# Stores on the queues of ScalarE and GpSimd, and sums products by contraction at two seams of a transformer block

## The chip, the cores and the metric

The kernel runs on one core of one Trainium2 chip. The metric is the device time of one execution in microseconds. Engines: PE is TensorE (matrix products), PEld its weight loads, DVE is VectorE, ACT is ScalarE, POOL is GpSimd, SP is SyncE, which up to now issues nearly all DMAs.

## The reference, cut to what matters

One layer of a hybrid block on a sequence of 1024 tokens with 1024 channels, all in 32-bit floats. The input is normalised and multiplied with one wide matrix w_in. Three branches follow: retention (4 heads), gated linear attention (4 heads) and sliding-window attention (16 query heads). They are projected, gated, summed, projected again and added to the input; then comes a gated feed-forward of width 2816.

```python
for l in range(DEPTH):                      # DEPTH = 1
    h = rmsnorm(x, norm_mix_pre[l])
    proj = h @ w_in[l]
    ...                                     # o_ret, o_gla, o_swa from slices of proj
    branches = jnp.stack([o_ret, o_gla, o_swa], axis=2)
    projected = jnp.einsum('bsnc,ncd->bsnd', branches, w_branch[l])
    gates = jax.nn.sigmoid(gate_logits.reshape(B, S, N_BRANCH, D_MODEL))
    merged = jnp.sum(gates * projected, axis=2)
    x = x + rmsnorm(merged @ w_out[l], norm_mix_post[l])
    h = rmsnorm(x, norm_ffn_pre[l])
    f = (jax.nn.silu(h @ ffn_w_gate[l]) * (h @ ffn_w_up[l])) @ ffn_w_down[l]
    x = x + rmsnorm(f, norm_ffn_post[l])
```

## The kernel before, in words

Every operand of a product is split into a high part (a cast on ScalarE, line 113) and a remainder (a subtraction, mostly on VectorE, line 114), and each product is three matmuls: high by high, high by low, low by high. `split` does this, `moving` does it into a new tile.

The stages follow one another in the listing. First the norm of x and its transposes; then the sliding-window branch, whose softmax steps are interleaved with projections (`swa_scores`, `swa_scale`, `swa_probs_t`, `swa_out`, up to some 325 us); then the eight heads of the two linear branches (`lin_head` and the functions around it, up to 784 us). Along the heads GpSimd also makes sums of blocks of the transposed input in `h_sums`, which are stored to DRAM as `tsum` and loaded again later.

Two stages then compute pairs of weight columns as 2 x 2 block products with seven products in place of eight: the class `Pairs`. It is used first for the gates (`gates`, 18 keys, a lead of 2 pairs) and later for the feed-forward's gate and up products (`up`, 22 keys, a lead of 3). For a key n the blocks a11, a12, a21, a22 come from two weight tiles `raw`. `blocks` splits the upper two, `sums` makes the sums s1 to s4 and splits s2 and s3, and `split` the others. The products are p1 (a11 by b11, into x), p2 (a12 by b21, into y), p6 (s2 by t2, onto x), p5 (s1 by t1, into z), p7 (s3 by t3, onto x), p4 (a22 by t4, onto x) and p3 (s4 by b22, onto z), each four contraction steps of three matmuls of 512 columns. `out` combines the results: in the gates `gate_out` (Silu or Sigmoid on ScalarE; for the six keys of heads a load of `on` and a product on VectorE at line 981; a store at line 982), in the feed-forward `up_out` (a store of fT at line 1166).

`Pairs.steps` writes the order out by hand. For the first `lead` keys it goes product by product: p1 and p2 of each key, then p6 of each, p5 of each, p7 of each, and so on; afterwards key by key. Two seams lead into these stages. At the first, the gates follow the last head, and the sums t1 to t4 are loaded from DRAM at line 989, sixteen loads of 512 KB. At the second, the output projection (`out_mm`, tiles t = 0 to 7), the norm of each tile (`out_norm`), the transposes of the normed tile (`out_transpose`, 64 copies h2f on ScalarE at line 1118) and the first feed-forward products are interleaved by hand; t2 and t1 are made there by `h2_t2` and `h2_t1`, when the last tile has been transposed.

The last stage is the down product (`down_load`, `down_mm`): for each half of the tokens it loads rows of w_down and of fT, and after the last block of each half it norms and stores four tiles of the output at line 1255.

The listing is not exactly the order in which an engine runs: the framework orders the instructions of each engine by priority (their place in the listing) and by its own estimate of when their inputs are ready, and adds the semaphores. Each engine and each DMA queue then runs its instructions in that order. SBUF tiles come from two pools: 18 of 512 columns (`bt`, `br_`) and 45 of 1024 (`dt_`, `bpair`, `raw_tile`, `wt_pair`). PSUM has eight banks of 512 columns (`bank`).

Of the kernel before, what the change touches and what calls it, by code (L numbers as in the profile page):

```python
# [16 lines left out]
P = 128  # L17
# [49 lines left out]
def block_kernel(ctx: ExitStack, tc: tile.TileContext, x, vecs, rows, alpha2, w_in, w_branch,  # L67
# [44 lines left out]
    def split(hi, lo, src, eng=None):  # L112
        se.copy(out=hi, in_=src)  # L113
        (eng or ve).tensor_tensor(out=lo, in0=src, in1=hi, op=ALU.subtract)  # L114
# [323 lines left out]
    def swa_out(i, pts):  # L438
# [13 lines left out]
        if n % 2 == 1:  # L452
            for c in range(2):
                sp.dma_start(out=oT[2][g * 2 + c][:, (n // 2) * 256:(n // 2 + 1) * 256], in_=oo[0][:, c, :])
# [154 lines left out]
    def lin_out(br, h, th, y, sgs):  # L609
        for i in range(2):  # L610
# [6 lines left out]
            if sgs is None:  # L617
# [5 lines left out]
                sp.dma_start(out=oN[br][c][:, th * TH:(th + 1) * TH], in_=ot)  # L623
# [8 lines left out]
            sp.dma_start(out=oT[br][c][:, th * TH:(th + 1) * TH], in_=ot)  # L632
# [128 lines left out]
    def h_sums(k):  # L761
# [7 lines left out]
        for n, src in (("t2", t2), ("t3", t3), ("t1", b22), ("t4", b21)):  # L769
            pr = dt_(n, F32R)  # L770
            split(pr[:, :TH], pr[:, TH:], src)
            sp.dma_start(out=tsum[n][k], in_=pr.bitcast(F32))
# [27 lines left out]
    class Pairs:  # L800
# [5 lines left out]
        def __init__(self, mv, keys, load, out, lead):  # L806
            self.mv, self.keys, self.load, self.out, self.lead = mv, keys, load, out, lead
            self.raw, self.ops, self.x, self.z, self.sn = {}, {}, {}, {}, {}
# [28 lines left out]
        def product(self, n, ps, a, b, start):  # L837
            wh, wl = self.ops[n].pop(a)
            if callable(self.mv[b]):
                self.mv[b] = self.mv[b]()  # L840
            for k, (hi, lo) in enumerate(self.mv[b]):
                h, l = wh[:, k * P:(k + 1) * P], wl[:, k * P:(k + 1) * P]
                pe.matmul(ps, lhsT=h, rhs=hi, start=(start and k == 0), stop=False, skip_group_check=True)  # L843
                pe.matmul(ps, lhsT=h, rhs=lo, start=False, stop=False, skip_group_check=True)  # L844
                pe.matmul(ps, lhsT=l, rhs=hi, start=False, stop=(k == KH - 1), skip_group_check=True)  # L845
# [6 lines left out]
        def p2(self, n):  # L852
            y = bank("y")
            self.product(n, y, "a12", "b21", True)
            self.out(n, 0, 0, y, self.sn[n].pop())
# [22 lines left out]
        def steps(self):  # L878
            keys, lead = self.keys, self.lead
            first = keys[:lead]  # L880
            self.fetch(lead)
            for i, n in enumerate(first):
                self.blocks(n)
                self.p1(n)
                yield
                self.p2(n)
                if i == 0:
                    self.sums(n)
                yield
            for i, n in enumerate(first):  # L890
                if i:
                    self.sums(n)
                self.p6(n)
                yield
            self.fetch(lead + 1)
            for n in first:
                self.split(n, "s1")
                self.p5(n)
                yield
            for n in first:  # L900
                self.p7(n)
                yield
            if lead < len(keys):
                self.blocks(keys[lead])
                self.p1(keys[lead])
                yield
            for n in first:
                self.split(n, "a22")
                self.p4(n)
                yield  # L910
            self.fetch(lead + 2)
            if lead < len(keys):
                self.p2(keys[lead])
                yield
            for i, n in enumerate(first):
                self.split(n, "s4")
                if i == len(first) - 1 and lead < len(keys):
                    self.sums(keys[lead])
                    self.split(keys[lead], "s1")
                self.p3(n)  # L920
                yield
# [47 lines left out]
    def gate_out(n, row, th, ps, add):  # L969
# [12 lines left out]
        sp.dma_start(out=(gT if gate else oT)[br][c + row][:, t], in_=g)  # L982
# [105 lines left out]
    def out_norm(t, ps, eng):  # L1088
# [8 lines left out]
        sp.dma_start(out=x1d[t], in_=x1)  # L1097
# [7 lines left out]
    def out_transpose(t, xn):  # L1105
# [5 lines left out]
        for k0 in range(0, NK, 4):  # L1111
# [14 lines left out]
    def h2_t2():  # L1126
        res = []
        for k in range(KH):
# [3 lines left out]
            res.append(moving("t2", t2))  # L1132
            tsums.append((t3, t2))
        return res
# [155 lines left out]
```

## Time and profile before

| | |
|---|---|
| median of 3 runs | 2230.48 us (2230.38 to 2238.79) |
| profiled execution | 2228.47 us, its span 2226.6 us, mean clock of TensorE 0.984 |
| busy time | PE 2141.1 us, PEld 1809.9, DVE 1188.7, ACT 867.2, POOL 215.8 |
| DMA | 274.32 MB, mean 123 GB/s, nearly all issued by SP |

The profiled execution is one run, 2.0 us under the median; the span is what the trace covers of it. A busy TensorE is not one at its peak: matmuls are pipelined, and a 512-column matmul that lasts 0.39 us in the trace starts 0.23 us after the one before it. At half clock (1.2 in place of 2.4 GHz, "0.50" in the granted clock) the distance is 0.43 us. The clock shown for a stretch is the mean of the two levels.

### The profile page before, as it was taken

The numbers are of one execution on the slowest core, as the hardware profiler recorded it, in microseconds if no ns is written. First come the engines' busy times: TensorE is split into PE (matmuls) and PEld (weight loads), VectorE is DVE, ScalarE is ACT, GpSimd is POOL, SyncE is SP. The second block draws the span as 40 slices with busy tenths as digits, with TensorE's granted clock in tenths as the row PEclk, the third lists the DMA queues.
The fourth block names the chain that finished last, engine by engine and source line by source line (L and its number), as shares of the span: only waits on it lengthen the run. The fifth ranks groups of instructions, "written<-read, shape, count | busy, mean of one in ns | idle before, by whom it ended". The sixth has DMA issues, their size and how long they took to land. (4 is left out here: it accounts for less than half of the span.)

```text
span 2226.6 us, 28111 instructions
## 1 busy us (share of the span) xinstructions
PE 2141.1 (96%) x10792; PEld 1809.9 (81%) x10792; DVE 1188.7 (53%) x2222; ACT 867.2 (39%) x1664; POOL 215.8 (10%) x244
## 2 busy tenths in 40 slices
PE   7999999999999969999999999996999999999998
PEld 6888889998889958888888888874788888888786
DVE  4699966766654446544532344334755555544351
ACT  4477643444443324444441220253433333343240
POOL 3221013333111100000000000030000000000000
PEclk9999999999999989999999999998899999999999
DMA  4011121122211358655462551232164444484450
GB/s 158 10 48 39 58 77 69 67 68 92 86 57 57 123 198 251 208 170 170 147 231 100 170 179 63 84 123 92 46 181 137 138 142 142 123 292 142 151 199 38
DMA packets 291845, 274.32 MB, mean 123 GB/s; under 512 B 11728, under 2 KB 240336, under 8 KB 291712
## 3 DMA queue, kind: packets, MB, share of 16 engines
q1 hardware_dynamic: 291664, 272.41, 37.6%
q8 instruction: 84, 1.38, 0.2%
q14 instruction: 49, 0.40, 0.1%
q0 software_dynamic: 48, 0.13, 0.0%
HBM read 212.73 MB, written 59.77 MB: 122 GB/s over the span
## 5 line engine op out<-in xcount | busy, mean ns | idle before, releaser
L114 DVE TENSOR_TENSOR wl<-raw,wh 128x1024 fp32r<-128x1024 f32 x138 | 168.4, 1221 | 164.8 <-ACT wh L113 88.1
L113 ACT CAST wh<-raw 128x1024 fp32r<-128x1024 f32 (+1 forms) x157 | 163.0, 1044 | 186.7 <-DMA raw<-in_w_branch 65.1
L226 PE MATMUL pf<-hT,wh 128*128 128x512 f32 x480 | 188.8, 393 | 3.6 <-DVE skl L114 1.8
L227 PE MATMUL pf<-hT,wh 128*128 128x512 f32 x480 | 188.3, 392 | 0.0
L229 PE MATMUL pf<-hT,wl 128*128 128x512 f32 x480 | 149.2, 391 | 1.3 <-POOL wl L114 1.3
L215 PE MATMUL pf<-o,wh 128*128 128x512 f32 x384 | 149.1, 389 | 0.0
L214 PE MATMUL pf<-o,wh 128*128 128x512 f32 x384 | 148.6, 389 | 0.0
L241 PE MATMUL v<-wh,hT 128*128 128x256 f32 x512 | 146.6, 286 | 0.0
L243 PE MATMUL v<-wh,hT 128*128 128x256 f32 x512 | 144.8, 283 | 0.0
L242 PE MATMUL v<-wl,hT 128*128 128x256 f32 x512 | 144.8, 283 | 0.0
L1072 POOL TENSOR_TENSOR rr<-rr,mhalf 128x1 f32<-128x1 f32 x16 | 8.6, 539 | 1380.2 <-DVE rr L1071 1380.2
L1221 PE MATMUL dn<-wh,f 128*128 128x512 f32 x352 | 136.8, 391 | 3.1 <-ACT f L113 3.1
L113 ACT CAST s<-raw 128x512 fp32r<-128x512 f32 x160 | 95.4, 621 | 111.0 <-DVE raw L822 50.9
L1222 PE MATMUL dn<-wl,f 128*128 128x512 f32 x352 | 137.0, 391 | 0.0
L843 PE MATMUL x<-t,s 128*128 128x512 f32 x320 | 127.8, 400 | 7.7 <-ACT s L113 4.8
L844 PE MATMUL x<-t,s 128*128 128x512 f32 x320 | 127.4, 398 | 1.6 <-DVE t L114 1.6
L797 ACT COPY sn<-x 128x512 f32<-128x512 f32 x120 | 70.3, 586 | 147.2 <-PE x L845 143.0
L845 PE MATMUL x<-t,s 128*128 128x512 f32 x320 | 126.8, 396 | 0.0
L217 PE MATMUL pf<-o,wl 128*128 128x512 f32 x384 | 118.8, 389 | 0.0
L114 DVE TENSOR_TENSOR s<-raw,s 128x512 fp32r<-128x512 f32 x160 | 106.7, 687 | 16.8 <-ACT s L113 16.2
L1224 PE MATMUL dn<-wh,f 128*128 128x512 f32 x352 | 109.4, 391 | 0.0
L226 PEld LDWEIGHTS pf<-hT,wh 128*128 128x128 f32 x480 | 90.8, 189 | 22.1 <-issue 3.0
(294 smaller groups left out, 5223.5 us busy)
## 6 DMA issues: line engine op xcount, KB each, us to landing
raw<-in_w_in SPq DMA_DIRECT2D x116, 512.0 KB, 4.6
raw<-in_w_down SPq DMA_DIRECT2D x44, 512.0 KB, 6.5
raw<-in_w_gate SPq DMA_DIRECT2D x43, 512.0 KB, 5.2
raw<-in_w_up SPq DMA_DIRECT2D x43, 512.0 KB, 6.1
t<-t SPq DMA_DIRECT2D x32, 512.0 KB, 5.2
raw<-in_w_branch SPq DMA_DIRECT2D x24, 512.0 KB, 6.0
gT<-go SPq DMA_DIRECT2D x48, 256.0 KB, 2.0
raw<-oT SPq DMA_DIRECT2D x24, 512.0 KB, 3.6
```

Of the source, the lines that this page charges most:

```text
L113: se.copy(out=hi, in_=src)
L114: (eng or ve).tensor_tensor(out=lo, in0=src, in1=hi, op=ALU.subtract)
L214: pe.matmul(p_, lhsT=wh, rhs=x2[th][0], start=(k == 0), stop=False)
L215: pe.matmul(p_, lhsT=wh, rhs=x2[th][1], start=False, stop=False)
L226: pe.matmul(p_, lhsT=wh, rhs=hi, start=(k == 0), stop=False)
L227: pe.matmul(p_, lhsT=wh, rhs=lo, start=False, stop=False)
L229: pe.matmul(p_, lhsT=wl, rhs=hi, start=False, stop=(k == NK - 1))
L241: pe.matmul(ps, lhsT=lh, rhs=rh, start=start, stop=False)
L242: pe.matmul(ps, lhsT=lh, rhs=rl, start=False, stop=False)
L243: pe.matmul(ps, lhsT=ll, rhs=rh, start=False, stop=stop)
L1221: pe.matmul(ps[ch], lhsT=fh[:, ts_], rhs=ws[ch][0], start=(first and i == 0), stop=False)
L1222: pe.matmul(ps[ch], lhsT=fh[:, ts_], rhs=ws[ch][1], start=False, stop=False)
```

## The change

It does five things.

1. Stores move from SP's queue to ACT's: lines 454, 623, 632, 982, 1097, 1166 and 1255, except those of the last tile. The stores of `tsum` at line 772 move to POOL's queue.
2. `Pairs` gets `products`, which runs one kind of product for several keys with the contraction step as the outer loop, so that for each step all keys use the same moving operand. `steps` uses it for s2, s1, s3, a22 and s4 of the first `lead` keys.
3. The outputs of p2 of the first keys are held back (`hold`) until after the s2 products; in the feed-forward they are also put behind the last t2 remainder on VectorE (`mark`, with `issue_after`, which orders them behind that instruction).
4. At the feed-forward seam the transposes of tiles 0 and 1 come at t = 3 and of tile 2 at t = 4 (before: all three at t = 4); the first key's blocks and sums come at t = 6 and t = 7 and the second's blocks ahead of the first product; the fetch of the third key no longer stands at t = 7; of the last tile's eight h2f copies four run on VectorE.
5. At the gate seam the third key's weights are fetched between the loads of t1 and t3.

```diff
     def split(hi, lo, src, eng=None):
         se.copy(out=hi, in_=src)
-        (eng or ve).tensor_tensor(out=lo, in0=src, in1=hi, op=ALU.subtract)
+        return (eng or ve).tensor_tensor(out=lo, in0=src, in1=hi, op=ALU.subtract)
...
-                sp.dma_start(out=oT[2][g * 2 + c][:, (n // 2) * 256:(n // 2 + 1) * 256], in_=oo[0][:, c, :])
+                se.dma_start(out=oT[2][g * 2 + c][:, (n // 2) * 256:(n // 2 + 1) * 256], in_=oo[0][:, c, :])
...
-                sp.dma_start(out=oN[br][c][:, th * TH:(th + 1) * TH], in_=ot)
+                se.dma_start(out=oN[br][c][:, th * TH:(th + 1) * TH], in_=ot)
...
-            sp.dma_start(out=oT[br][c][:, th * TH:(th + 1) * TH], in_=ot)
+            se.dma_start(out=oT[br][c][:, th * TH:(th + 1) * TH], in_=ot)
...
-            sp.dma_start(out=tsum[n][k], in_=pr.bitcast(F32))
+            po.dma_start(out=tsum[n][k], in_=pr.bitcast(F32))
...
         def product(self, n, ps, a, b, start):
-            wh, wl = self.ops[n].pop(a)
+            self.products([n], [ps], a, b, start)
+
+        def products(self, ns, pss, a, b, start):
+
+            ws = [self.ops[n].pop(a) for n in ns]
+            self.make(b)
+            for k, (hi, lo) in enumerate(self.mv[b]):
+                for ps, (wh, wl) in zip(pss, ws):
+                    h, l = wh[:, k * P:(k + 1) * P], wl[:, k * P:(k + 1) * P]
+                    pe.matmul(ps, lhsT=h, rhs=hi, start=(start and k == 0), stop=False, skip_group_check=True)
+                    pe.matmul(ps, lhsT=h, rhs=lo, start=False, stop=False, skip_group_check=True)
+                    pe.matmul(ps, lhsT=l, rhs=hi, start=False, stop=(k == KH - 1), skip_group_check=True)
+
+        def make(self, b):
             if callable(self.mv[b]):
                 self.mv[b] = self.mv[b]()
...
-        def p2(self, n):
+        def p2(self, n, hold=False):
             y = bank("y")
             self.product(n, y, "a12", "b21", True)
+            if hold:
+                return lambda: self.out(n, 0, 0, y, self.sn[n].pop(0))
             self.out(n, 0, 0, y, self.sn[n].pop())
...
             self.fetch(lead)
+            held = []
             for i, n in enumerate(first):
-                self.blocks(n)
+                if n not in self.ops:
+                    self.blocks(n)
                 self.p1(n)
                 yield
-                self.p2(n)
-                if i == 0:
+                held.append(self.p2(n, True))
+                if "s2" not in self.ops[n]:
                     self.sums(n)
                 yield
-            for i, n in enumerate(first):
-                if i:
-                    self.sums(n)
-                self.p6(n)
-                yield
+            self.make("t2")
+            self.products(first, [x[n] for n in first], "s2", "t2", False)
+            for h in held:
+                if self.mark:
+                    with tc.issue_after(self.mark[0].ins):
+                        h()
+                else:
+                    h()
+            for n in first:
+                self.sn[n].append(snap(x[n]))
+            yield
             self.fetch(lead + 1)
+            self.make("t1")
             for n in first:
                 self.split(n, "s1")
-                self.p5(n)
-                yield
-            for n in first:
-                self.p7(n)
-                yield
+                z[n] = bank("z")
+            self.products(first, [z[n] for n in first], "s1", "t1", True)
+            yield
+            self.products(first, [x[n] for n in first], "s3", "t3", False)
+            self.make("t4")
...
-        sp.dma_start(out=(gT if gate else oT)[br][c + row][:, t], in_=g)
+        se.dma_start(out=(gT if gate else oT)[br][c + row][:, t], in_=g)
...
             for n in ("t2", "t1", "t3", "t4"):
-                mv[n] = mv[n]()
+                if n == "t3":
+                    gates.fetch(3)
+                gates.make(n)
...
-        sp.dma_start(out=x1d[t], in_=x1)
+        se.dma_start(out=x1d[t], in_=x1)
...
-                se.activation(out=h2f[k][th][:, ts_], in_=src, func=AF.Copy, scale=g)
+                if t == NT - 1 and k >= KH:
+                    ve.tensor_scalar(out=h2f[k][th][:, ts_], in0=src, scalar1=g, scalar2=None, op0=ALU.mult)
+                else:
+                    se.activation(out=h2f[k][th][:, ts_], in_=src, func=AF.Copy, scale=g)
...
-            res.append(moving("t2", t2))
+            pr = bpair("t2")
+            last = split(*pr, t2)
+            res.append(pr)
             tsums.append((t3, t2))
+        up.mark.append(last)
...
-        sp.dma_start(out=fT[f][:, th * TH:(th + 1) * TH], in_=o)
+        se.dma_start(out=fT[f][:, th * TH:(th + 1) * TH], in_=o)
...
         ps, = out_mm((t,))
+        if t == 3:
+            out_transpose(0, xns.pop(0))
+            out_transpose(1, xns.pop(1))
         if t == 4:
-            for t2 in range(3):
-                out_transpose(t2, xns.pop(t2))
+            out_transpose(2, xns.pop(2))
         if t == 5:
+            up.fetch(1)
             out_transpose(3, xns.pop(3))
-            up.fetch(1)
-            mv["b11"] = mv["b11"]()
-            mv["b21"] = mv["b21"]()
+            up.make("b11")
+            up.make("b21")
         if t == 6:
+            up.blocks(0)
             up.fetch(2)
             out_transpose(4, xns.pop(4))
         if t == 7:
-            up.fetch(3)
+            up.sums(0)
             out_transpose(5, xns.pop(5))
         xns[t] = out_norm(t, ps, po if t < NT - 1 else ve)
+    up.blocks(1)
     next(ups)
...
-                sp.dma_start(out=out[t * P:(t + 1) * P, cs], in_=o[ch])
+                (sp if t == NT - 1 else se).dma_start(out=out[t * P:(t + 1) * P, cs], in_=o[ch])
```

## Rows read from the trace of the kernel before

**Rows 1.** Busy us (count) by stretch: PE, PEld, DVE, ACT, POOL; PEclk, DMA share, GB/s.

```profile
75.00:325.00 250.00, 245.65 (x1410) 212.35 (x1409) 209.19 (x667) 165.02 (x475) 39.83 (x29) 1.00 0.15 43
...
784.20:816.30 32.10, 15.10 (x57) 11.05 (x57) 14.49 (x23) 5.84 (x9) 0.99 (x1) 0.79 0.72 265
816.30:1440.00 623.70, 623.70 (x2750) 515.50 (x2749) 285.23 (x418) 203.32 (x324) 0.00 (x0) 1.00 0.51 162
...
1511.70:1589.40 77.70, 57.27 (x200) 40.67 (x198) 46.88 (x71) 33.59 (x71) 1.88 (x4) 0.78 0.19 57
...
2105.00:2113.40 8.40, 5.30 (x15) 3.81 (x15) 3.65 (x4) 3.13 (x4) 0.00 (x0) 0.80 1.04 409
```

**Rows 2.** Waits of TensorE: us in total, times, longest us.

```profile
PE x L843 <- ACT wh L113: 15.2, 4, 9.4
...
PE pr L1082 <- ACT h2f L1118: 3.8, 2, 3.5
PE dn L1221 <- ACT f L113: 3.1, 1, 3.1
```

**Rows 3.** Timeline of SyncE's DMA issues before the gate seam: start, us.

```profile
765.95 1.76 SPq L989 DMA_DIRECT2D t<-t  x4
791.39 0.98 SPq L632 DMA_DIRECT2D oT<-ot  x2
792.46 8.20 SPq L989 DMA_DIRECT2D t<-t  x12
...
801.58 0.32 SPq L980 DMA_DIRECT2D on<-oN  x1
```

**Rows 4.** Gate seam: timeline with waits in brackets, and one stretch of busy time.

```profile
786.18 0.50 PE L843 MATMUL x<-hT,wh 128*128 128x512 f32 x1 [1.88 <-ACT wh L113]
...
798.19 0.50 PE L843 MATMUL x<-t,s 128*128 128x512 f32 x1 [3.57 <-ACT s L113]
...
811.30 0.69 DVE L981 TENSOR_TENSOR go<-go,on 128x512 f32<-128x512 f32 x1 [11.63 <-DMA on<-oN]
...
813.19 0.80 PE L845 MATMUL x<-hT,wl 128*128 128x512 f32 x1 [10.69 <-DVE wl L114]
...
802.00:806.00 4.00, 0.50 (x2) 0.00 (x0) 0.00 (x0) 0.00 (x0) 0.00 (x0) 0.93 1.02 419
```

**Rows 5.** Busy time by stretch, inside the output projection.

```profile
1466.00:1485.00 19.00, 14.51 (x67) 11.40 (x66) 4.55 (x8) 10.04 (x37) 7.67 (x10) 0.91 0.31 109
```

**Rows 6.** Timeline of TensorE at the feed-forward seam.

```profile
1521.31 0.80 PE L843 MATMUL x<-b,wh 128*128 128x512 f32 x1 [9.37 <-ACT wh L113]
...
1553.50 0.79 PE L843 MATMUL x<-t,s 128*128 128x512 f32 x1 [2.83 <-ACT t L113]
```

**Rows 7.** Busy time by stretch, while t2 and t1 are made.

```profile
1560.00:1580.00 20.00, 18.36 (x60) 13.13 (x60) 17.23 (x29) 13.03 (x24) 0.00 (x0) 0.74 0.09 25
```

**Rows 8.** Timeline of SyncE and ScalarE at the second half of the down product.

```profile
2087.31 4.27 SPq L1255 DMA_DIRECT2D out<-o  x4
...
2098.31 1.19 SPq L1213 DMA_DIRECT2D rf<-fT  x2
...
2106.61 1.04 ACT L113 CAST wh<-raw 128x1024 fp32r<-128x1024 f32 x1 [3.73 <-DMA raw<-in_w_down]
```

**Rows 9.** The page's costliest groups, VectorE: count, busy us, mean ns.

```profile
L114 DVE TENSOR_TENSOR wl<-raw,wh 128x1024 fp32r<-128x1024 f32 x138 | 168.4, 1221 | 164.8 <-ACT wh L113 88.1
...
L114 DVE TENSOR_TENSOR s<-raw,s 128x512 fp32r<-128x512 f32 x160 | 106.7, 687 | 16.8 <-ACT s L113 16.2
```

**Rows 10.** SyncE's stores: ns min/median/max of one issue, and its longest waits.

```profile
L454 SPq DMA_DIRECT2D oT<-oo x32: 319/383/979, 114.3 to 322.6; - x32
...
SPq L1166 <- DVE fo L1165: 283.2, 44, 19.8
SPq L454 <- DVE oo L451: 228.9, 16, 43.4
```

**Rows 11.** Timeline of GpSimd after the sums of one block.

```profile
385.10 0.56 POOL L706 TENSOR_SCALAR tu<-tu,vec 128x256 f32<-128x256 f32 x1 [16.36 <-DVE tu L695]
```

More of the change, by code (lines that the diff above doesn't have):

```diff
@@ L807, in __init__ @@
             self.mv, self.keys, self.load, self.out, self.lead = mv, keys, load, out, lead
-            self.raw, self.ops, self.x, self.z, self.sn = {}, {}, {}, {}, {}
+            self.raw, self.ops, self.x, self.z, self.sn, self.mark = {}, {}, {}, {}, {}, []
         def fetch(self, upto):
@@ L837, in product @@
         def product(self, n, ps, a, b, start):
-            wh, wl = self.ops[n].pop(a)
+            self.products([n], [ps], a, b, start)
[9 more added lines that the diff above has]
+        def make(self, b):
             if callable(self.mv[b]):
                 self.mv[b] = self.mv[b]()
[L841 to L845, printed above, removed]
         def p1(self, n):
@@ L880, in steps @@
             first = keys[:lead]
+            x, z = self.x, self.z
             self.fetch(lead)
+            held = []
             for i, n in enumerate(first):
-                self.blocks(n)
+                if n not in self.ops:
+                    self.blocks(n)
                 self.p1(n)
                 yield
-                self.p2(n)
-                if i == 0:
+                held.append(self.p2(n, True))
+                if "s2" not in self.ops[n]:
                     self.sums(n)
@@ L895, in steps @@
+            yield
             self.fetch(lead + 1)
+            self.make("t1")
             for n in first:
                 self.split(n, "s1")
-                self.p5(n)
-                yield
-            for n in first:
-                self.p7(n)
-                yield
[L903 to L906, printed above, removed]
+                z[n] = bank("z")
+            self.products(first, [z[n] for n in first], "s1", "t1", True)
@@ L907, in steps @@
+            yield
+            self.products(first, [x[n] for n in first], "s3", "t3", False)
+            self.make("t4")
             for n in first:
                 self.split(n, "a22")
-                self.p4(n)
-                yield
+                self.out(n, 1, 1, z[n], snap(x[n]))
+            yield
+            nxt = keys[lead] if lead < len(keys) else None
+            if nxt is not None:
+                self.blocks(nxt)
+                self.p1(nxt)
+                yield
+            self.products(first, [x[n] for n in first], "a22", "t4", False)
@@ L911, in steps @@
+            for n in first:
+                self.split(n, "s4")
+                self.out(n, 1, 0, x.pop(n), None)
+            yield
             self.fetch(lead + 2)
-            if lead < len(keys):
-                self.p2(keys[lead])
+            if nxt is not None:
+                self.p2(nxt)
+                self.sums(nxt)
+                self.split(nxt, "s1")
                 yield
[L915 to L921, printed above, removed]
+            self.products(first, [z[n] for n in first], "s4", "b22", False)
@@ L922, in steps @@
+            for n in first:
+                self.out(n, 0, 1, z.pop(n), self.sn.pop(n).pop())
+                del self.raw[n], self.ops[n]
+            yield
             if lead < len(keys):
```

## The prediction

> **What bounds the kernel now.** I read the busy time by stage first. Between 816.3 and 1440 us TensorE issues 2750 matmuls in 623.7 us without a gap: 0.2268 us each [rows 1], the pitch used below for a 512-column matmul. Nothing on another engine matters in such a stretch, so the only time to win is where TensorE stands still or runs slow. The ranking of TensorE's waits says where: the weight casts and remainders of block products, the transposed copies h2f, the operands of the down product [rows 2]. They fall into four places.
>
> Gate seam, 784.2 to 816.3: 57 matmuls, 16 of them 128-column transposes (8 take some 0.75 us). 41 x 0.2268 + 1.5 = 10.8 us of work in 32.1 us: 21.3 us lost, at a mean clock of 0.79 [rows 1]. The reader should see three pieces. The first product waits 1.88 us for its weight cast, and the third 0.64 for the remainder. The first sums product waits 3.57 us for its cast. Then one matmul waits 10.69 us for a remainder wl on VectorE; VectorE itself had stood 11.63 us for the load "on" [rows 4]. That load was issued at 801.58 behind twelve 512 KB loads of sums [rows 3] while the DMA engines ran flat out at 419 GB/s [rows 4]. The twelve had themselves stood on SyncE behind two stores, which left at 791.39; four earlier loads had gone at 765.95 [rows 3].
>
> Output projection, 1466 to 1485: 4.5 us idle at a clock of 0.91 [rows 5]. Here 24 h2f copies in a row hold the PSUM banks that the next tile needs [rows 2]. A clock share of 0.91 of 19 us is 3.4 us at the 1.2 GHz level, some 8 matmuls at 0.43 us in place of 0.23, so 1.6 us more: 6.1 us.
>
> Feed-forward seam, 1511.7 to 1589.4: 77.7 us for 180 wide matmuls and 16 transposes, 42.3 us of work: 35.4 us lost, clock 0.78 [rows 1]. Its waits are 9.37 us until 1521.31 for the first weight cast, which stands on ScalarE behind the last tile's norm, and 2.83 us for the first sum t2 at 1553.50 [rows 6]. After that the t2 remainders come one by one from VectorE, which is busy 17.23 of 20 us [rows 7].
>
> Down product, 2105.0 to 2113.4: 3.1 us idle, then 5.2 us at the slow level for 12 matmuls that need 2.7: 5.6 us lost [rows 1, 2]. SyncE issued the output stores first and the rf loads only at 2098.31; ScalarE waited 3.73 us for w_down [rows 8].
>
> Sum of the four: 68.4 us.
>
> **The change part by part.** The order of instructions on an engine is set by the framework's own estimate of readiness, not by the listing alone, so I cost resources and not an exact order.
>
> *Gate seam.* The two oT stores leave SyncE, so the twelve loads no longer stand behind them; they are bounded then by free slots, which the end of the last head gives at about 781.5 (the end of its last output products). With the two weight loads moved between t1 and t3 that is 14 x 512 KB = 7.3 MB, at 419 GB/s 17.5 us: done near 799 to 800, before "on" is wanted. The outputs of the first pairs, the additions, Silu, loads of "on" and stores, come after the s2 products, so the late "on" no longer stands ahead of the second pair's wl. What is late next: both pairs' s2 splits, because a contraction-outermost run needs all of them at its start. VectorE's work up to that point is two wl (1.22 each), eight sums and four remainders (0.69 each) and four ot (0.72) [rows 9]: 2.4 + 8.3 + 2.9 = 13.6 us from 786.3, hence about 800 without gaps, and TensorE has 48 matmuls, 10.9 us, from 786.2 on. The first wait, 2.5 us, is unchanged. Bounds: 19 us won if only that stays; 6 if slots keep the loads late and VectorE meets "on" again behind the s2 products. I take 13, since the earlier loads and the held outputs each work against the 10.69 us, while slots are short (the first four loads waited for them too).
>
> *Output projection.* Two transposes move to tile 3, one to tile 4. Two need four banks, beside tile 3's two and tile 4's two: eight. ScalarE makes 16 copies before tile 3's squares and not 24 after its norm. Bounds 3 to 6; I take 6, because all of this wait hangs on that one group.
>
> *Feed-forward seam.* blocks(0) and sums(0) go under the products of tiles 6 and 7, blocks(1) ahead of the first product. The 9.37 us therefore falls away: TensorE has 72 matmuls (16.3 us) and 16 transposes (1.5 us) to do while tile 7 goes through its norm, and the first t2 remainder, about 14.8 us after tile 7's products (the norm's chain took 10.4 us, transposes and copies 2.2, two sums, a cast and a remainder 2.2), is ready before it is needed at 17.8. The order by contraction gives the next remainder 9 x 0.2268 = 2.0 us, and VectorE makes one in 1.8 (three operations at 0.6). VectorE is then the bound: 46.9 us of its work lie in the stage [rows 1], 5.3 of them (1.22 + six at 0.69 [rows 9]) moved ahead, 41.6 left; at the busiest share the stage shows, 0.86 [rows 7], that is 48.4 us, plus 2 for the start of the chain: 50.4 in place of 77.7, 27 won. Bounds: 33, if VectorE hides under 42.3 us of TensorE plus 2; 9, if VectorE keeps its old share of 0.60 (41.6 / 0.60 = 69). Four of the last tile's eight copies on VectorE shorten ScalarE's part by about 1 us, inside this. The moved up.fetch(3) takes two loads from ahead of tile 7's x.
>
> *Down product.* Stores of tiles 0 to 3 on ScalarE leave SyncE free for rf and w_down from 2085 or earlier, 13 us ahead of 2098.31. 5.5 won, bounds 3 and 5.6.
>
> The Trainium skill (page "DMA: Bandwidth & Descriptors", section "Issuing engines are not separate DMA queues") speaks against the moved stores: all queues end on the same 16 DMA engines, and a second issuing engine saves only the sequencer's issue time. The rows show another thing at 2087 to 2098, a load that waited in order behind a store that waited for VectorE [rows 8]; by the rule alone this part would be worth nothing.
>
> *What it costs.* 202 stores go to ScalarE: 32 at L454, 8 at L632, 24 at L623, 72 at L982, 8 at L1097, 44 at L1166, 14 at L1255. The trace shows no store on ScalarE; the nearest row is SyncE's, 0.38 us median [rows 10]. So 0 to 77 us of ScalarE's own time, in the page's 867 of 2226. Each store also waits in order for its data, with casts, snaps and exponentials queued behind it, for which VectorE and then TensorE wait. In the middle stretches TensorE ran on while ScalarE was a third busy, so I hide it there. In 75 to 325, with VectorE at 209 and ScalarE at 165 of 250 us [rows 1], 32 stores add 12 us and the cover is thin: 3 us on the path, 0 to 12. 16 stores go to GpSimd, behind which L706 waits, needed by the next chunk; it had 16.36 us of room [rows 11]. Four stores would have to take over 4 us each; 1 us, 0 to 4. Elsewhere 1 us. Costs together 5, bounds 0 to 16.
>
> **The sum** is made against the profiled execution, 2228.5 us (span 2226.6 and 1.9 around it): 2228.5 - 13 - 6 - 27 - 5.5 + 5 = 2182. The median of the runs is 2.0 above that execution, so 2184.
>
> **The rivals.**
> (a) VectorE and slots still bind the seams: gains 6, 6, 12 and 5.5 at cost 5. Time 2228.5 - 24.5 + 2 = 2206. For it: the row of t2 remainders [rows 6, 7], already one by one; against: half the lost time there lies before t2 exists.
> (b) The moves gain nothing but free SyncE: the scheduler interleaves as before; 5.5 and 6 won, 5 lost: 2224. For it: matmuls of different pairs are already interleaved at 799 to 802. Against: the weights of the first pair are listed a whole tile earlier.
> (c) Slower: ScalarE pays SyncE's waits. SyncE stood 283 us ahead of L1166 and 229 ahead of L454 [rows 10], 512 together. If a tenth of that reaches TensorE, 51 us, the gain of 51.5 is gone; at 15 per cent, 77 us, the time is 2228.5 - 51.5 + 77 + 2 = 2256. Against: SyncE stood there because it had nothing else to do, ScalarE arrives later.
> (d) Queues save only issue time: the down product wins nothing and the gate loads come no sooner (8 in place of 13): 2228.5 - 8 - 6 - 27 + 5 + 2 = 2194. The rule of the skill named above would have it so. Against: rows 3 and 8.
>
> **How the numbers follow.** Forecast 0.52, (a) 0.24, (b) 0.10, (c) 0.06, (d) 0.08. A measurement of this kernel tells about 0.5 per cent, 11 us, from no change. Faster by more: forecast, (a), (d), 0.84; within: (b), 0.10; slower: (c), 0.06. All gains at their upper bounds and no cost give 2228.5 - 63.6 + 2 = 2167; (a) with costs near their upper bound gives 2214. The range is 2167 to 2214, and leaves out (b), (c) and little else.
>
> **What would show it.** Gate seam: no wait over 4 us on TensorE, t loads issued before 791, "on" off the path. Feed-forward seam: x from b starts at once after the last out product, the s2 products of three pairs begin some 18 us later. Down product: no wait for w_down. ScalarE shows DMA issues and no PE wait on an exponential or a cast behind one. It would be wrong if a new wait on ScalarE's casts stood in the middle stretches, or if the list order put the late load ahead of a split again.

## The result, and the profile after

The changed kernel takes 2200.23 us (median of 4 runs, 2198.55 to 2202.22) against 2230.43 us: a ratio of 0.9856, 95% interval 0.9831 to 0.9881, faster by some 30 us, 1.4 per cent. The prediction was 2184, its range 2167 to 2214. The profiled execution has a span of 2200.1 us against 2226.6, 26.5 less.

Where these 26.5 us come from is read from the first and last start of a few matmul groups, which cut the span into stages of equal work. Of the kernel after (count, ns min/median/max, first and last start):

```profile
L241 PE MATMUL kv<-vh,n x56: 277/278/388, 330.3 to 773.3; 128*128 128x256 f32 x56
...
L241 PE MATMUL o<-us,q x56: 279/283/386, 334.8 to 777.5; 128*128 128x256 f32 x56
...
L214 PE MATMUL pf<-o,wh x384: 389/389/389, 1133.7 to 1399.5; 128*128 128x512 f32 x192
...
L1110 PE MATMUL pr<-row,mg x128: 389/389/796, 1400.4 to 1499.5; 128*128 128x512 f32 x128
...
L1259 PE MATMUL dn<-wh,f x352: 389/389/504, 1946.2 to 2189.3; 128*128 128x512 f32 x176
```

The same starts in before and in two experiments told below give this table (us; the spread is that of the profiled executions in which the stage has the same code as after):

| stage | before | after | after - before | stores only | order only | spread |
|---|---|---|---|---|---|---|
| start to the first key cast (skh) of the sliding window | 64.3 | 68.5 | +4.2 | 68.2 | 68.6 | 64.3 to 68.6 |
| sliding window, to its last output product | 254.8 | 255.1 | +0.3 | 255.2 | 256.2 | 255.1 to 256.0 |
| heads: first kv to last head product | 455.2 | 447.2 | -8.0 | 447.1 | 452.7 | 447.1 to 447.3 |
| gate stage with its seam, to the first pf<-o | 364.0 | 356.2 | -7.8 | 362.7 | 357.0 | 354.8 to 358.6 |
| output projection: first to last pr | 98.3 | 99.1 | +0.8 | 94.9 | 98.6 | 98.4 to 99.3 |
| feed-forward with its seam, to the first dn | 461.7 | 446.7 | -15.0 | 463.3 | 448.7 | 446.7 to 448.5 |
| down product: first to last dn | 244.0 | 243.1 | -0.9 | 244.2 | 243.2 | 243.1 to 248.7 |

The first row is no part of the change: with unchanged code the executions fall at 64.3 to 65.3 or at 68.2 to 68.6. In the slower ones the granted clock of 20 to 40 and 40 to 60 us is lower (0.81 and 0.87 in after, 0.89 and 1.00 in before). Without this row the profiled executions differ by 30.7 us, as the medians do.

What is left of the waits of [rows 2], and two stretches that answer to [rows 1]: the feed-forward seam, taken as 77.7 - 15.0 = 62.7 us from the last pr on, and ten us of the second half of the down product (busy us (count) of PE, PEld, DVE, ACT, POOL, clock, DMA share, GB/s):

```profile
PE x L847 <- ACT s L113: 7.0, 2, 4.3
PE z L847 <- ACT s L113: 6.3, 1, 6.3
PE x L847 <- ACT wh L113: 6.0, 2, 4.1
...
PE pr L1110 <- ACT h2f L1149: 3.5, 1, 3.5
PE dn L1259 <- ACT f L113: 3.2, 2, 2.9
...
1499.50:1562.20 62.70, 51.20 (x214) 40.07 (x213) 47.89 (x77) 35.94 (x75) 2.10 (x5) 0.89 0.16 51
...
2076.00:2086.00 10.00, 7.10 (x31) 5.22 (x30) 2.90 (x4) 1.88 (x3) 0.00 (x0) 1.00 0.98 366
```

No wait of 9 or 10 us is left in the two seams. But there are four of 2.8 to 6.3 us, all on casts of ScalarE; h2f still costs 3.5 us and the down product still stands 2.9 us.

### The profile page after: what moved, and what is told of

It is laid out like the page before. It is cut to its first block, busy times and chain, and to the rows that moved or that the text cites. A ratio compares the mean times of both kernels' runs of the same rounds, so it can differ in the third digit from the quotient of the medians.

```text
span 2200.1 us, 28003 instructions
## 1 busy us (share of the span) xinstructions
PE 2134.7 (97%) x10792; PEld 1811.0 (82%) x10792; DVE 1186.4 (54%) x2226; ACT 870.2 (40%) x1660; POOL 222.8 (10%) x260
## 5 line engine op out<-in xcount | busy, mean ns | idle before, releaser
L847 PE MATMUL x<-t,s 128*128 128x512 f32 x320 | 124.5, 393 | 7.3 <-ACT s L113 7.0
L848 PE MATMUL x<-t,s 128*128 128x512 f32 x320 | 125.6, 392 | 0.1
L849 PE MATMUL x<-t,s 128*128 128x512 f32 x320 | 124.8, 390 | 0.0
## 6 DMA issues: line engine op xcount, KB each, us to landing
gT<-go ACTq DMA_DIRECT2D x48, 256.0 KB, 2.0
```

## The experiments

Seven of the runs below put one edit, or two, on the kernel after; none of them has a ratio whose interval is clear of the change's own (0.9831 to 0.9881). The two kernels with five and six edits, told last, come out at its edge. What a single edit did is therefore read from the stages and waits of one profiled execution, beside the spread in the table.

**Stores and order apart.** Two kernels split the change: one is before with the moved stores alone, the other after with every moved store back on SyncE.

```diff
-   sp.dma_start(out=oT[2]...)   and those of oN, oT, gT/oT, x1d, fT, and out but for its last tile
+   se.dma_start(out=oT[2]...)
-   sp.dma_start(out=tsum[n][k], ...)
+   po.dma_start(out=tsum[n][k], ...)
```

This is stores only; order only is the reverse, on the kernel after.

> The kernel before with all eight moves of stores and nothing else. Theory Q (the queues gain in the eight heads, where the two traces differ by 8.1 us between the first and the last head product, 455.5 against 447.4): about 2222 us, first to last head product near 447, both block seams within 3 us of before. Rival S (ScalarE pays elsewhere what SyncE gains): 2230, ratio 1.00 plus or minus 0.003, with waits of TensorE on casts that stand behind a store. Rival O (the 8.1 us come from another order of the listing and not from the queues): 455 between the head products and 2230.

> The changed kernel with every moved store back on SyncE. Theory Q: the seams keep their gains (gate seam 7.7, feed-forward seam 15.0 us between landmarks of the two traces) and the heads lose 8.1, so some 2230.4 - 7.7 - 15 = 2208. If the stores ahead of the casts on ScalarE are what holds the seams back (4.3 us at 795, 2.8 at 1577, and the slow clock behind each), the seams gain more and it ends at 2196 to 2202, level with the changed kernel. If the twelve loads of sums need SyncE free of stores, the gate seam gains nothing and it ends near 2215.

Stores only: 2219.5 us, ratio 0.9949 (0.9935 to 0.9963). Order only: 2211.7 us, ratio 0.9914 (0.9896 to 0.9932). Their gains, 12 and 20 us, come to about the change's 30. Theory Q holds: the heads' 8 us come with the stores (447.1) and mostly go without them (452.7); both seams come with the order. Rival S falls as a whole. One thing neither theory said: the output projection takes 94.9 us with the stores alone, and 99.1 when the order is added. The order's 20 us are not split further at the seams: the first key's early blocks and sums, the held outputs, the third key's fetch and the four copies on VectorE were not taken back one by one.

How a store kept the heads waiting is seen in before. SyncE held four oN stores from 612.86 on, which waited for ScalarE, and the next weight load left behind them at 627.80. ScalarE then waited 2.44 us for that load with the casts vh and us queued behind its wh, and TensorE stood. Timelines of SyncE and ScalarE, and busy us (count) of PE, PEld, DVE, ACT, POOL, clock, DMA share and GB/s:

```profile
612.86 14.83 SPq L623 DMA_DIRECT2D oN<-ot  x4
627.80 0.39 SPq L134 DMA_DIRECT2D raw<-in_w_in  x1
...
631.87 1.05 ACT L113 CAST wh<-raw 128x1024 fp32r<-128x1024 f32 x1 [2.44 <-DMA raw<-in_w_in]
...
630.00:640.00 10.00, 7.61 (x31) 6.06 (x30) 4.06 (x9) 3.87 (x6) 0.56 (x1) 0.83 0.61 197
```

In after the loads left at 594.37 and from 608.85 on, the cast starts without a wait, and the same stretch is nearly full at full clock:

```profile
594.37 0.37 SPq L134 DMA_DIRECT2D raw<-in_w_in  x1
608.85 16.42 SPq L145 DMA_DIRECT2D raw<-in_w_in  x2
...
630.47 1.05 ACT L113 CAST wh<-raw 128x1024 fp32r<-128x1024 f32 x1
...
630.00:640.00 10.00, 9.55 (x51) 8.07 (x50) 6.17 (x12) 4.37 (x8) 2.28 (x3) 1.00 0.19 53
```

**The stores of tsum alone** (before, with line 772 changed and nothing else).

```diff
-            sp.dma_start(out=tsum[n][k], in_=pr.bitcast(F32))
+            po.dma_start(out=tsum[n][k], in_=pr.bitcast(F32))
```

> The kernel before with the 16 stores of block sums on GpSimd's queue and nothing else. If these stores, which wait for GpSimd's sums in SyncE's order ahead of the heads' weight loads, are what the heads' 8.1 us come from: 2222 and 447 us between first and last head product. If it is the heads' own stores, or none of both: 2230 and 455.

2233.0 us, ratio 1.0 (0.9987 to 1.0013): in the whole time nothing. The heads take 451.6 us, 3.6 less than in before but only 1.1 less than with order only, where no store moved (452.7), so less than half of the heads' gain is in these sixteen stores. The waits tell more: of the six that TensorE has in the heads of before (over 0.4 us each), the four ahead of 600 us, 2.8 us together, are gone, and the two after 630, of 1.9 and 1.0 us here, stay. These are the ones behind the oN stores shown above.

**Ten seam stores on GpSimd.**

```diff
-   se.dma_start(out=oT[br][c][:, ...], in_=ot)
+   (po if (br, h) == (1, H - 1) else se).dma_start(out=oT[br][c][:, ...], in_=ot)
-   se.dma_start(out=fT[f][:, ...], in_=o)
+   (po if f < 3 else se).dma_start(out=fT[f][:, ...], in_=o)
```

> The changed kernel with ten stores taken off ScalarE and given to GpSimd, which is idle there: the last head's four oT stores and the six fT stores of the first three feed-forward keys; the orders of TensorE and VectorE stay as they are. Theory (a store that waits for its data holds the casts behind it): the wait of 4.3 us for the first s2 cast at 795 shrinks below 1, that of 2.8 us at 1577.7 goes, with the slow clock after each some 4 + 4 = 8 us less than the changed kernel, 2192. Rival (the casts would have come no sooner, since VectorE's sums or the slots bind): within 2 us of the changed kernel, 2200.

2196.7 us, ratio 0.9845 (0.9827 to 0.9863), which overlaps the change's own. The theory mostly falls: the waits became 3.1 (from 4.3) and 2.8 us (unchanged). In after, ScalarE had waited 5.31 us with a store of ot in front of the cast; without the store it waits 6.50 us for VectorE's sum, which stands in VectorE's row behind ot, and ot waits for the transposes on TensorE. Timelines of after (TensorE, ScalarE, VectorE, SyncE):

```profile
795.35 0.76 PE L847 MATMUL x<-t,s 128*128 128x512 f32 x1 [4.29 <-ACT s L113]
...
787.82 4.63 ACTq L632 DMA_DIRECT2D oT<-ot  x4
792.50 0.62 ACT L113 CAST s<-raw 128x512 fp32r<-128x512 f32 x1 [5.31 <-DVE ot L630]
...
790.66 1.41 DVE L630 SCALAR_TENSOR_TENSOR ot<-yt,vec,sg 128x512 f32<-128x512 f32 x2 [2.20 <-PE yt L613]
...
762.39 9.06 SPq L1015 DMA_DIRECT2D t<-t  x8
789.86 1.07 SPq L982 DMA_DIRECT2D raw<-in_w_in  x2
791.03 10.56 SPq L1015 DMA_DIRECT2D t<-t  x8
```

and with the ten stores on GpSimd (ScalarE, SyncE):

```profile
794.08 0.62 ACT L113 CAST s<-raw 128x512 fp32r<-128x512 f32 x1 [6.50 <-DVE raw L824]
...
760.20 6.25 SPq L1015 DMA_DIRECT2D t<-t  x8
767.49 2.94 SPq L982 DMA_DIRECT2D raw<-in_w_in  x2
770.52 7.93 SPq L1015 DMA_DIRECT2D t<-t  x8
```

SyncE's rows hold what nobody had asked: the loads of sums, which in after stop until 789.86, are all out by 778.5 once the last head's stores leave ScalarE, although SyncE's own order is the same. After's list of waits says what held them: SyncE waited 18.6 us ahead of the third key's weight loads for stores of oT.

```profile
SPq L982 <- DMA oT<-ot: 18.6, 2, 18.3
```

The instruction list of the compiled kernel gives the link. The framework counts every DMA of SyncE and ScalarE on eight completion semaphores in turn, and an instruction that takes one waits first for its last user (DMAHW is a semaphore of these two queues, DMASW one of GpSimd's):

```
79 L1015 DMA t_1299_8284<-t_3_3564 128x1024 [waits DMAHW6_49,DMASW7_49,PE_49]
80 L982 DMA raw_8286<-in_w_in 128x8x128 [waits DMAHW7_49,PE_49]
```

The last DMA ahead of this load that counts on DMAHW7 is a store of oT from the last head, on ScalarE, and so the load waited for it. The Trainium skill gives a reason for such a wait (page "DMA: Bandwidth & Descriptors", section "Why a DMA increments its semaphore by 16 and not by 1"): two DMAs in flight on one semaphore can't be told apart, so each needs its own. No run here lets two share one; what the trace shows is the price of keeping them apart, this wait of 18.3 us and one of 34.6 us below.

**The output stores of tiles 0 to 3 on GpSimd.**

```diff
-   (sp if t == NT - 1 else se).dma_start(out=out[...], in_=o[ch])
+   (sp if t == NT - 1 else po if t < 4 else se).dma_start(out=out[...], in_=o[ch])
```

> The changed kernel with the eight stores of output tiles 0 to 3 on GpSimd's queue in place of ScalarE's. Theory L (the loads of the second half wait on SyncE for those stores all the same, because the framework counts loads of SyncE and stores of ScalarE on the same eight completion semaphores in turn; GpSimd's have their own): SyncE's first rf load leaves before 2050 and not at 2064.8, TensorE's wait of 2.9 us at the second half goes, and the down product takes 238 to 240 us in place of 243.1. Rival B (DMA engines, which run flat out there, or the tiles' slots, bind): rf earlier, but 242 to 245 all the same.

2196.1 us, ratio 0.9848 (0.9831 to 0.9865); the down product takes 239.0 us, and 240.6 in each of the two runs told last, which have this edit too. All three lie below its other executions with the code of after (243.1 to 248.7). Theory L holds for the first loads of fT (rf). In after, two of them left at 2027.36 and 2029.89, not one at 2064.8 as the expectation has it, and the third stood 34.6 us, until 2064.84, for a store on ScalarE. With the stores on GpSimd ten had left by 2037.7, and TensorE's wait on f is gone from its list. Waits and timeline of SyncE in after, then with the stores on GpSimd:

```profile
SPq L1251 <- DMA out<-o: 39.4, 5, 34.6
...
2027.36 2.85 SPq L1251 DMA_DIRECT2D rf<-fT  x2
...
2064.84 0.98 SPq L1251 DMA_DIRECT2D rf<-fT  x2
```

```profile
SPq L1251 <- DMA out<-o: 39.0, 6, 27.0
...
2022.78 2.63 SPq L1251 DMA_DIRECT2D rf<-fT  x4
2026.86 0.33 SPq L1249 DMA_DIRECT2D raw<-in_w_down  x1
2028.09 3.48 SPq L1251 DMA_DIRECT2D rf<-fT  x4
...
2036.82 29.05 SPq L1251 DMA_DIRECT2D rf<-fT  x4
```

But rival B is right in part, with the tiles' slots. SyncE's loads waited 39.0 us in all for the stores on GpSimd too, 27.0 of them ahead of the eleventh load of fT. In the compiled kernel that load waits for GpSimd's first output store, and its tile has the SBUF address of the output tile that this store reads (24064). A wait for a place in SBUF goes with the store to any queue. The gain came from what could leave ahead of it.

**The splits ahead of the held outputs** (after; t1 and the first keys' s1 split are listed before the held p2 outputs, not behind them).

```diff
+           self.make("t1")
+           for n in first: self.split(n, "s1")
            for h in held: ...
...
-           self.make("t1")
            for n in first:
-               self.split(n, "s1")
                z[n] = bank("z")
```

> The changed kernel with t1 and the first keys' s1 split listed ahead of the held outputs of p2, at both seams. Theory H (the held outputs with their table load and three Silus stand on ScalarE ahead of the t1 and s1 casts, and TensorE waits 6.28 us for them at 1543): that wait falls to 1 or less and the matmuls after it keep the full clock, 6 to 8 us less from the last out-projection matmul to the first of the down product (446.7 becomes 439 to 441), 2193 in all. Rival V (VectorE, which makes t1 and the remainders, is full there and the wait only moves): 444 to 447 and 2198 to 2201.

2195.3 us, ratio 0.9856 (0.9839 to 0.9873), in the whole time level with after; feed-forward 443.3, between the upper theory's 441 and the rival's 444, and 443.4 and 444.0 in the two runs told last. The wait of 6.28 us became 2.83 and the later one of 2.76 became 2.81. What stood in front of the casts is seen in after: a table load, three Silus and two snaps after the last s2 product, then t1, then s1.

```profile
1536.06 0.59 ACT L797 COPY sn<-x 128x512 f32<-128x512 f32 x1 [1.98 <-PE x L849]
1536.66 1.28 ACT L1191 ACT_TABLE_LOAD   x1
1537.95 1.67 ACT L1191 ACTIVATE fo<-fo 128x512 f32<-128x512 f32 x3
1539.53 1.05 ACT L797 COPY sn<-x 128x512 f32<-128x512 f32 x2
1540.47 2.18 ACT L113 CAST t<-t 128x512 fp32r<-128x512 f32 x4
1542.55 1.66 ACT L113 CAST s<-raw 128x512 fp32r<-128x512 f32 x3
...
1543.22 0.80 PE L847 MATMUL z<-t,s 128*128 128x512 f32 x1 [6.28 <-ACT s L113]
```

**Key by key** (after, with the two loops of `products` exchanged).

```diff
-            for k, (hi, lo) in enumerate(self.mv[b]):
-                for ps, (wh, wl) in zip(pss, ws):
+            for ps, (wh, wl) in zip(pss, ws):
+                for k, (hi, lo) in enumerate(self.mv[b]):
```

> The changed kernel with the loops of products exchanged: each key's product is finished before the next key's begins; everything else stays. If the order by contraction step is what the feed-forward seam gained by: the t2 remainders come 2.4 us apart and the first key would need all four in 2.7 us, so TensorE stands some 5 us in the s2 products, at a slow clock after it, and the stage goes from 446.7 to 452 or more, 2206 in all. If the wait of 6.28 us that follows absorbs it, because ScalarE's casts of t1 and s1 end at the same time in either order: 447 to 449, 2200 to 2203.

2204.0 us, ratio 0.9889 (0.9873 to 0.9906); feed-forward 446.4, the same as after. The rival's number came, but not its reason: in the compiled list the 36 s2 products of the three feed-forward keys stand in the same order as in after, contraction step outermost. The framework put them so by its estimate of when each t2 is ready, and only the later products went key by key. So the run says only that the order of the later products isn't what the seam gained by, and that the new loop isn't needed for the order of s2; what the other order of s2 would have cost isn't shown.

**The transposes as before** (after, with tiles 0 to 2 transposed at t = 4).

```diff
-        if t == 3:
-            out_transpose(0, ...); out_transpose(1, ...)
         if t == 4:
-            out_transpose(2, xns.pop(2))
+            for t2 in range(3): out_transpose(t2, xns.pop(t2))
```

> The changed kernel with the transposes of tiles 0, 1 and 2 all at t = 4, as in the kernel before. Theory T (moving two of them to t = 3 gained nothing: the stores alone brought the output projection from 98.3 to 94.9 us and the moves took it back to 99.1): 95 us from the first to the last out-projection matmul, 2196 in all. Rival (the 99.1 come from the first key's blocks and sums at t = 6 and t = 7, which share VectorE and ScalarE with the norms): 99 again, 2200.

The output projection takes 94.9 us, as with the stores alone: theory T holds for the stage. TensorE's wait on h2f there is 1.1 us, as with the stores alone; in after it is 3.5. The whole is 2200.1 us, ratio 0.9878 (0.9858 to 0.9898), no faster than after: the feed-forward took 1.8 us more (a weight cast 5.2 us late, in after 4.1) and the down product 5.6 more, in code that is the same.

**The gate operands early** (the ten stores on GpSimd, and the first two gate keys' blocks and sums listed ahead of the last head's closing steps).

```diff
+    gates.fetch(2)
+    for n in gkeys[:2]:
+        gates.blocks(n)
+        gates.sums(n)
     for i, _ in enumerate(gates.steps()):
```

> The kernel with ten stores on GpSimd (2196.7), and in addition the blocks and sums of the first two gate keys listed ahead of the last head's closing steps. Theory D (what holds the first s2 cast is VectorE's order: the sums stand behind the last head's ot, which waits for its transposes on TensorE): the 3.1 us wait at 794.8 goes, with some 2 us of slow clock behind it; 354.9 us from the last head product to the first projection product become 349 to 351, 2192 in all. Rival (the last head's closing steps now come late and hold banks and SBUF tiles): 355 or more, 2197 or more.

2201.6 us, ratio 0.9876 (0.9859 to 0.9892). The wait on s went, but one of 3.1 us on a snap of ScalarE took its place; the gate stage took 352.6 us, 2.3 less than with the ten stores alone, which the spread of this stage can't tell from nothing. Inconclusive in time; that the sums' place in VectorE's row held the first s2 cast is shown.

**The second key's blocks early** (after, with `up.blocks(1)` ahead of `out_norm` of the last tile).

```diff
+        if t == NT - 1:
+            up.blocks(1)
         xns[t] = out_norm(t, ps, po if t < NT - 1 else ve)
-    up.blocks(1)
```

> The changed kernel with the blocks of the second feed-forward key listed ahead of the last tile's norm. Theory N (the cast of its weights stands on ScalarE behind the last tile's x1 store and square, which wait for the norm): TensorE's 4.1 and 1.0 us waits at 1511.9 and 1513.8 fall to under 1 together, with 2.5 us of slow clock behind them, and the feed-forward stage takes 440 to 442 us in place of 446.7. Rival (TensorE then only reaches the last transposes and the t2 remainders sooner and waits there): 445 to 447.

2198.3 us, ratio 0.9856 (0.984 to 0.9872), feed-forward 445.7. The rival holds: the waits of 4.1 and 1.0 us went, and TensorE stood 4.3 us for the last tile's xn in their place.

```profile
PE h2t L1142 <- DVE xn L1130: 4.3, 1, 4.3
```

**Together, and the sums on GpSimd.** The five edits in one kernel (ten seam stores and the output stores on GpSimd, splits first, transposes as before, second blocks early); then with the s1 and s4 sums of the first three feed-forward keys on GpSimd as well, which is this edit:

```diff
+            eng = po if self.lead == 3 and n in self.keys[:3] else ve
-            ve.tensor_tensor(out=a21, in0=a21, in1=a22, op=ALU.add)
-            ve.tensor_tensor(out=a12, in0=a12, in1=a11, op=ALU.subtract)
+            eng.tensor_tensor(out=a21, in0=a21, in1=a22, op=ALU.add)
+            eng.tensor_tensor(out=a12, in0=a12, in1=a11, op=ALU.subtract)
```

> The changed kernel with five edits: ten seam stores on GpSimd, the s1 and t1 splits ahead of the held outputs, the three transposes at t = 4, the output stores of tiles 0 to 3 on GpSimd, the second key's blocks ahead of the last norm. If the parts add (1.3, 2.4 + 3.4, 4.2, 4, 5 us by the stages of the single runs, the last two as theories L and N would have it): 2200 - 20 = 2180. If they hide behind one another as at the feed-forward seam, where one wait took over from another: 2188 to 2192.

> The kernel with the five edits, and the sums for s1 and s4 of the first three feed-forward keys (six additions of 0.69 us, four of them in VectorE's row without a gap between the last xn and the end of t2) on GpSimd, which is idle there. Theory V (VectorE's amount of work between the last tile's norm and t2 sets when the s2 products can run): the s2 products start 2 to 3 us sooner, the feed-forward stage takes 440 to 441 us in place of 443.4, 2186 in all. Rival N (the norm's chain and the order around the last transposes set it): the stage stays at 443 to 444, 2189.

Together: 2189.0 us, ratio 0.9812 (0.9794 to 0.983). That is the case of parts that hide behind one another (2188 to 2192). By stages: gate 354.1, output projection 95.0, feed-forward 443.4, down product 240.6. The output projection keeps its 4 us and the down product 2.5 of its 4.1; in the feed-forward two edits that alone gave 3.4 and 1.0 gave 3.3 together, since one wait took over from another there (TensorE stands 5.3 us for the last tile's xn). With the sums: 2187.1 us, 0.9811 (0.9791 to 0.9831), feed-forward 444.0. Rival N's number came, but the run doesn't clear VectorE: GpSimd is late itself, its first addition of 1.29 us stands ahead of the last norm's rr, and the last xn begins 17.9 us after the last pr (1487.6 to 1505.5) in place of 16.5 (1493.4 to 1509.9).

```profile
1498.41 1.29 POOL L827 TENSOR_TENSOR raw<-raw 128x512 f32<-128x512 f32 x1 [2.49 <-DVE rr L1101]
1499.65 0.55 POOL L1102 TENSOR_TENSOR rr<-rr,mhalf 128x1 f32<-128x1 f32 x1
```

## Why the prediction was right, and where its steps were not

The time lay in the range and the order of the parts was right: the feed-forward seam first, the gate seam next. But the likeliest value was 16 us too low, and its terms were less right than their sum: gains at the four places were forecast as 51.5 us and measured as 22.9 (7.8 - 0.8 + 15.0 + 0.9), and the item put down as a cost of 5 was a gain of 7.7 in the heads and the sliding window. That this made up 12.7 of the 28.6 us that were missing is luck: the prediction did not see it.

*Gate seam: 13 forecast, 7.8 measured.* The mechanism was right in that "on" and the second pair's wl no longer hold TensorE for 10.69 us [rows 4]. The step that failed is that the loads "no longer stand behind" the stores: moved to ScalarE they still held the loads, through the shared semaphores, until 789.86. This cost little, though. With the loads out by 778.5 the stage gained 1.3 us, inside its spread. What mostly held the first s2 product, 4.29 us against the sign of "no wait over 4 us", is the sums behind ot on VectorE, where the prediction had counted VectorE "without gaps". With the sums early this wait went, but a snap took its place, and no gain is clear of the spread.

*Output projection: 6 forecast, 0.8 lost.* The step "all of this wait hangs on that one group" failed: two groups in place of one still left a wait of 3.5 us. Here the gain is the moved stores' (in this stage x1's alone move), 3.4 us, for which nothing was put down; moving the transposes took 4.2 back, as their return shows (94.9).

*Feed-forward seam: 27 forecast, 15.0 measured, inside the bounds of 9 to 33.* The 9.37 us of [rows 6] did fall away, and x from b starts at once, at 1501.20. Three steps of this part failed.

The first is the overlap with the last tile's norm. TensorE's 72 matmuls and 16 transposes were to take 17.8 us; they took 27.3 (1500.41 to 1527.72). TensorE waited 4.08 and 1.00 us in them for the second key's weights, whose cast stands on ScalarE behind the last tile's x1 store and square, and the granted clock from 1511.87 to 1519 was 0.52. The chain to the first t2 remainder, put at "about 14.8 us after tile 7's products", was long too: it ended at 1528.01, after 27.6 us, since xn is done at 12.2, not at 10.4, and VectorE then goes through the second and third key's weights and sums. But TensorE, as late itself, did not stand for it, and its list of waits has none on t2. With the second key's blocks early the wait only moved, to 4.3 us for xn: the chain is the next thing to bind. Timelines of TensorE, ScalarE and VectorE in after:

```profile
1500.41 1.03 PE L1142 MATMUL h2t<-ident,xn 128*128 128x128 f32 x8
...
1511.87 0.52 PE L847 MATMUL x<-b,wh 128*128 128x512 f32 x1 [4.08 <-ACT wh L113]
...
1513.81 0.80 PE L849 MATMUL x<-b,wl 128*128 128x512 f32 x1 [1.00 <-DVE wl L114]
...
1527.72 0.84 PE L847 MATMUL x<-t,s 128*128 128x512 f32 x3
...
1509.36 0.33 ACTq L1125 DMA_DIRECT2D x<-x  x1
1509.74 1.06 ACT L1128 ACTIVATE xn<-x 128x1024 f32<-128x1024 f32 x1 [1.31 <-DVE x L1124]
...
1510.79 1.03 ACT L113 CAST wh<-raw 128x1024 fp32r<-128x1024 f32 x1
...
1511.87 0.76 DVE L1130 TENSOR_SCALAR xn<-x,rstd 128x1024 f32<-128x1024 f32 x1 [2.54 <-POOL rstd L127]
...
1527.32 0.69 DVE L114 TENSOR_TENSOR t<-t,t 128x512 fp32r<-128x512 f32 x1
```

The second is ScalarE's order after the s2 products, which the tally left out: the held outputs' Silus ahead of the t1 and s1 casts, for which TensorE waited 6.28 us. Moving these gave back 3.4 us of the stage.

The third is VectorE's work, taken as 41.6 us at a share of 0.86. The 62.7 us that answer to the stretch still hold 47.89 us of it, at a share of 47.89 / 62.7 = 0.76.

*Down product: 5.5 forecast, 0.9 measured.* "Leave SyncE free" failed: from the third load of fT on, the loads stood 39.4 us for the stores on ScalarE in place of the same stores on SyncE. (Before's first two such loads, which the prediction passed over, left at 2091.64 and 2095.39, ahead of its 2098.31.) On GpSimd's queue the gain came, 4.1 us, or 2.5 with the other edits.

*Costs: 5 forecast, 7.7 gained.* In the sliding window, where 3 were taken, +0.3. In the heads the trace of before held a gain that the prediction did not look for: SyncE's stores waited in order ahead of weight loads there as well.

Of the rivals, (a) with 2206 and (d) with 2194 lie nearer to 2200 than the forecast does. (a)'s 6 and 12 us at the two seams are close to the 7.8 and 15.0, and VectorE's row does stand without a gap through much of the second; its "6 won" in the output projection and its cost of 5 failed like the forecast's. (b) is out by the order-only run (20 us gained with all stores on SyncE), (c) by the stores-only run (12 us gained). (d) forecast the gate seam's 8 and the down product's nothing, for another reason. The Trainium skill's rule (page "DMA: Bandwidth & Descriptors", section "Issuing engines are not separate DMA queues"), that a second issuing engine saves only the time to issue, doesn't cover this: here a queue change moved the third load of fT from 2064.84 to 2024.28, by what waits in order and on which semaphore, and the heads' gain is the stores' alone.

## What to carry to other kernels

Before a store is moved to another queue to free loads, look in the compiled list at which completion semaphores both use, and at which loads go into the tiles that the stores still read: ScalarE's stores held SyncE's loads here by a shared semaphore, GpSimd's only those that wanted a tile's place. When work is listed earlier at a seam, cost the whole row of each engine that makes operands, in its order, up to each operand that TensorE needs next, not the stage's mean share. And look for stores that wait ahead of loads in the stages without a visible stall too: a quarter of this change's gain lay there.

## What had not been expected of the hardware

With the same code the first 70 us of the program took 64.3 to 65.3 us in some executions and 68.2 to 68.6 in the others, with a mean clock of 0.89 in one of the former and 0.81 in one of the latter in the stretch of 20 to 40 us. From 40 to 60 us it is 1.00 in all six of the former and 0.86 or 0.87 in all eight of the latter. The down product with its stores on SyncE or ScalarE took 242.1 to 248.7 us, with waits of TensorE on f of 2.2 to 6.5 us, while its loads run the DMA engines flat out (share 0.98 to 1.04, up to 418 GB/s). What makes the wait differ from run to run isn't shown. A difference of a few us in one profile of these two stages means nothing by itself.
